# Down groups set apart, moves and taps in three steps, and halved sums in a two-layer decoder trunk

## The chip, the cores and the metric

The kernel runs on one core of a Trainium2 chip. Its engines each work through their own queue in order: PE (TensorE, matrix products; its weight loads are shown as PEld), DVE (VectorE), ACT (ScalarE), POOL (GpSimd) and SP (SyncE, which here only issues DMAs). The metric is the device time of one execution in microseconds (us); lower is better. The time before is 2166.23 us, the median of 3 runs (2166.11 to 2166.46).

## The reference

The input has 256 tokens of 2048 features in float32. Two layers follow each other: one with a pooling mixer, one with dilated attention over a shared K and V. After each mixer comes a gated feed-forward block with a causal convolution of width 3, and after each of the four blocks a layer norm of the scaled stream. The change lies in and around the feed-forward block:

```python
def conv_ffn(h, w_up, conv_w, conv_b, w_down):
    u = h @ w_up
    up = jnp.pad(u, ((0, 0), (CONV_WIDTH - 1, 0), (0, 0)))
    c = conv_b + up[:, 0:S] * conv_w[0]
    for j in range(1, CONV_WIDTH):
        c = c + up[:, j:j + S] * conv_w[j]
    gate, val = jnp.split(c, 2, axis=-1)
    return (jax.nn.silu(gate) * val) @ w_down
...
        h = layer_norm(DEEPNORM_ALPHA * h + mix, ln1_g[i], ln1_b[i])
        ff = conv_ffn(h, ffn_w_up[i], ffn_conv_w[i], ffn_conv_b[i], ffn_w_down[i])
        h = layer_norm(DEEPNORM_ALPHA * h + ff, ln2_g[i], ln2_b[i])
```

`w_up` is 2048 by 11008 (gate and value halves of 5504), `w_down` is 5504 by 2048.

## The kernel before

**Units.** All weights are cut into units, mostly 512 rows by 512 columns (1 MB in float32). The list `units` holds them in the order in which PE takes them, and `run_units` (L125) writes the instructions of every engine unit by unit: `ahead` (L110) issues the load of the unit five further on and the split of the unit three further on; then come the unit's products; then the functions that `later` (L119) has put off to this unit; then the unit's own post function. `later(n, f)` means: n units from here. As every engine keeps this order in its queue, an instruction that waits holds up all that were written behind it on its engine. There are three raw buffers for loads and four buffers for split weights.

**Split.** Every float32 operand is used as a high part (rounded to the matrix format) and a low part (the rest). For a weight unit, `do_split` (L74) lets ACT cast the high part (`wh`, L82) and DVE subtract it from the raw weights (`wl`, L83). Each product is then made as high by high, high by low and low by high. In an up unit (L164 and L165) the activations' two parts lie side by side, so it takes 16 pairs of products of width 512 and 256.

**Seven products.** Down units of certain quads are done with seven block products in place of eight. `split_sums` (L90) makes two units of one weight tile. The "a" unit has ACT cast the left columns and the lower right block (L101) and DVE subtract (L103); then DVE reorders the raw blocks in place by four subtractions (L105 to L108). The "b" unit has ACT cast the whole reordered tile (L95) and DVE subtract it (L96). `mk_seven` (L196) gives three products to the "a" unit and four to the "b" unit (18 and 24 instructions; L223 to L225), the latter in the order: right token block by a left-column block into `t1` (it uses `wh` and `wl` in `N1`), then the sums number 2, 0 and 1 into `s3` and `s2`. The sums of the left operand (`xs`) come from `left_sums` (L617): four additions, and a function one unit later with four casts and four subtractions.

**Feed-forward block.** The 5504 hidden features are cut into quads of four 128-blocks (quad 10 has three). `up(q, mid, end)` (L666) places the gate group of quad q (four up units), then the groups in `mid`, the value group (four up units) and the groups in `end`. After a gate group, `evac` (L564) copies the products out through two scratch buffers (tag `t1`; ACT L576, DVE L577); one unit later `conv` (L580) runs all three taps: four activations for the middle tap (L585), four each for the other two (L590), each pair closed by a DVE addition (L591); one unit later follow sigmoid and product. A value group goes the same way, is multiplied by its gate (L654) and, one unit or more later, is split into the quad tile `gq[q]` (L282, L286), with its left sums. The quads are grouped into chunks (0-2, 3-5, 6-7, 8-10). When a chunk's quads are there, its down products run as four down groups (one for each 512 output columns) between the up groups of the next chunk. A down group of the first two chunks has five units (one ordinary, two pairs of "a" and "b"), one of the third chunk four.

The order around the change, in the first two chunks: gate q, first down group, value q, second down group, gate q+1, third and fourth down group, value q+1. In the third chunk every down group already stands between two up groups. The table `wait` holds back the split of a value quad until the quad tiles of the chunk before are free. After each down group with seven products (of the first three chunks), POOL adds three tiles onto the token stream by accumulating transfers (L267).

**Block moves.** For the down products the stream is turned from features on partitions to tokens on partitions and back: a DVE transpose of 32 by 32 blocks into `hb` and 16 DMAs on SP that put the blocks in place. `to_tokens` (L722) issues its 16 DMAs one unit after the transpose, `to_features` (L743) its 16 in two units, eight each. They are started by `lo` in `chain` (L423) and by `tm_post` (L784). `masks` (L1094) builds the attention masks in the feed-forward block of layer 0.

Of the kernel before, what the change touches and what calls it, by code (L numbers as in the profile page):

```python
# [32 lines left out]
def trunk(ctx: ExitStack, tc: tile.TileContext, x, pool_w_in, pool_w_grp, pool_scale, pool_w_out,  # L33
# [56 lines left out]
    def split_sums(i, kind):  # L90
        h = wh[i] = wp.tile([P, 4, 512], F32R, name=f"wh{i}", tag="wh")
        l = wl[i] = wp.tile([P, 4, 512], F32R, name=f"wl{i}", tag="wl")
        if kind == "b":
            r = raw.pop(i - 1)
            A.copy(h, r)  # L95
            V.tensor_tensor(l, r, h.bitcast(F32), OP.subtract)  # L96
            return
        r = raw[i]
        parts = [(slice(0, 4), N1), (B2, N2)]
        for k, n in parts:  # L100
            A.copy(h[:, k, n], r[:, k, n])  # L101
        for k, n in parts:
            V.tensor_tensor(l[:, k, n], r[:, k, n], h[:, k, n].bitcast(F32), OP.subtract)  # L103
# [3 lines left out]
        V.tensor_tensor(r22, r22, r11, OP.subtract)  # L107
        V.tensor_tensor(r21, r21, r22, OP.subtract)  # L108

    def ahead(i):  # L110
# [77 lines left out]
    def group_tm(w, r0s, c0, ncol, xqs, post, apart=False, seven=(), early=None):  # L188
# [7 lines left out]
        def mk_seven(kind, j):  # L196
            fst, fin, op, cl = j == 0, j == len(r0s) - 1, j == opening, j == closing

            def go(h, l):
# [9 lines left out]
                def sm(i):  # L209
                    return lambda hl, kk: sums[i][:, hl, kk, :]  # L210
# [186 lines left out]
    def chain(ps, lay, which, after):  # L397
# [149 lines left out]
    def ffn(lay):  # L547
# [7 lines left out]
        if lay == 1:  # L555
            sevens[9] = (0, 2)
        wait = {}

# [5 lines left out]
        def evac(ps, nb, mode):  # L564
# [3 lines left out]
            def tmp():  # L568
                return fp.tile([P, T], F32, name="ut", tag="t1", bufs=2)

# [8 lines left out]

        def conv(u, blk0, nb):  # L580
            cv = cvec[lay]
            c = pools["ffn"].tile([P, 4, T], F32, name="c", tag="t4")
            for m in range(nb):
                j = blk0 + m
                A.activation(c[:, m, :], u[:, m, 2:], AF.Identity, scale=cv[:, 2, j:j + 1], bias=cv[:, 3, j:j + 1])  # L585
            a = pools["ffn"].tile([P, 4, T], F32, name="a", tag="t4")
            for i, to in ((1, a), (0, u[:, :, 0:T])):
                for m in range(nb):
                    j = blk0 + m
                    A.activation(to[:, m, :], u[:, m, i:i + T], AF.Copy, scale=cv[:, i, j:j + 1])  # L590
                V.tensor_tensor(c[:, :nb], c[:, :nb], to[:, :nb], OP.add)  # L591
            return c

# [5 lines left out]
        def gate_chain(q, nb, mode, ps):  # L599
                u = evac(ps, nb, mode)  # L600

                def two():
                    c = conv(u, 4 * q, nb)

                    def three():
# [6 lines left out]

                later(1, two)

        def left_sums(q, s):  # L617
            pool, tag = (hp, "h") if q in (2, 5, 7) else (lnp, "sq")
            two = pool.tile([P, 2, 2, 2, P], F32R, name="xs01", tag=tag)
            one = pools["ffn"].tile([P, 2, 2, P], F32R, name="xs2", tag="xs", bufs=2)  # L620
            if len(sevens[q]) < 4:
                own = pools["ffn"].tile([P, 2, 2, P], F32R, name="xs3", tag="xs", bufs=2)
            else:
                own = gq[q][:, 0:2, :, P:T].rearrange("p k h t -> p h k t")
            xs[q] = [two[:, 0], two[:, 1], one, own]
            a11, a12, a21, a22 = (s[:, k:k + 2, t * P:t * P + P] for k, t in ((0, 0), (2, 0), (0, 1), (2, 1)))
# [20 lines left out]
        def val_chain(q, nb, mode, ps):  # L647
            u = evac(ps, nb, mode)

            def two():  # L650
                c = conv(u, NF + 4 * q, nb)

                s = gates.pop(q)
# [7 lines left out]

                later(wait.get(q, 1), three)

            later(0 if q in (2, 5, 7, 10) else 1, two)

# [37 lines left out]
        wait[9] = len(d[3]) - 1  # L703
        up(8, d[:1], d[1:2])
        up(9, d[2:3], d[3:])
        up(10, (), ())
        mark = len(units)
# [14 lines left out]
    def to_tokens(q):  # L722
# [5 lines left out]

        def move():
            ht = hp.tile([P, 4, T], F32, name="ht", tag="h")  # L730
            v = ht.rearrange("p a t -> p (a t)").rearrange("p (t c) -> p t c", t=2)
            to = ht.rearrange("p m t -> p (m t)").rearrange("p (k a j) -> p a k j", k=8, a=4)
            fr = hf.rearrange("p (k b j) -> p b k j", k=8, b=4)
            for a in range(4):
                for b in range(4):
                    nc.sync.dma_start(to[32 * b:32 * b + 32, a], fr[32 * a:32 * a + 32, b])
            HT[q] = v

        later(1, move)

    def to_features(c):  # L743
# [3 lines left out]

        def move(part):
            if part == 0:
                H[c] = hp.tile([P, 4, T], F32, name="h", tag="h")  # L750
            to = H[c].rearrange("p m t -> p (m t)").rearrange("p (k a j) -> p a k j", k=8, a=4)
            fr = hf.rearrange("p (k b j) -> p b k j", k=8, b=4)
            for a in (2 * part, 2 * part + 1):
                for b in range(4):
                    nc.sync.dma_start(to[32 * b:32 * b + 32, a], fr[32 * a:32 * a + 32, b])

        later(1, lambda: move(0))
        later(2, lambda: move(1))


# [23 lines left out]
    def tm_post(lay, n, c):  # L784
# [305 lines left out]
    with tc.tile_pool(name="ffn0", bufs=4) as fp:  # L1090
# [3 lines left out]
        def masks(i):  # L1094
            two = fp.tile([P, 2, P], F32, name="dist", tag="t1", bufs=2)
# [3 lines left out]
            itwo = fp.tile([P, 2, P], I32, name="idist", tag="t1", bufs=2)  # L1099
            idist, im = itwo[:, 0], itwo[:, 1]  # L1100
# [10 lines left out]
        for i in range(3):  # L1111
            later(56 + 3 * i, lambda i=i: masks(i))
        run_units(marks[1])
# [35 lines left out]
```

## Time and profile before

| what | value |
|---|---|
| median of 3 runs | 2166.23 us |
| the profiled execution | 2164.68 us |
| its span, first to last instruction | 2162.9 us |
| DMA traffic | 405.90 MB, mean 188 GB/s |
| casts of whole weight tiles, L82 (ACT, 128x2048) | 286 of 1906 ns |
| subtractions of whole weight tiles, L83 (DVE, 128x2048) | 286 of 2288 ns |

The profile is taken from one execution. Busy time counts an engine's own instructions; matrix products are pipelined, so their durations overlap and PE's busy time says only when it had something in flight. A group's row ends with the engine's idle time just before these instructions and who ended most of it. A window's row gives the busy time of each engine in a stretch, the TensorE clock that was granted there (1.00 is full) and the DMA engines' share. In rows of the timeline, the bracket at the end is the idle time before the instruction and its releaser; "SPq" is SP's DMA queue.

### The profile page before, as it was taken

To read this page: it belongs to the slowest core of one execution; us is meant where nothing else is said; L and a number is where in the kernel's file an instruction comes from. 1 tells how busy PE (TensorE), PEld (TensorE's weight loads), DVE (VectorE), ACT (ScalarE), POOL (GpSimd) and SP (SyncE) were. 2 spreads that over 40 slices of the span, in tenths; PEclk is the share of its full clock that TensorE was granted. 3 is DMA by queue.
4 is the path that set the end of the run, shared out by engine and by line. 5 is a ranking of instruction groups with operands and counts; after the bars stand their busy time and mean duration, and the time that the engine had idled before them with its cause. 6 is when DMAs were issued, how large, how long until landed. Compare 5 with 4: busy or idle time off the path is not lost.

```text
span 2162.9 us, 30852 instructions
## 1 busy us (share of the span) xinstructions
PE 2068.3 (96%) x12388; PEld 1834.3 (85%) x12388; DVE 1678.5 (78%) x1971; ACT 1236.1 (57%) x1612; POOL 75.3 (3%) x112
## 2 busy tenths in 40 slices
PE   9999999898999889989999999999898999899999
PEld 8899987787888788879888888988688888788887
DVE  6768876887888788679856667787788778878878
ACT  6444776565665566456544444576655665665652
POOL 1000000001000000000000000000000000000000
PEclk9999999999999999999999999999999999999999
DMA  8655466556555646675566554557475647546465
GB/s 262 214 181 189 156 196 190 184 190 205 184 166 190 210 149 207 172 213 175 182 203 190 167 193 166 173 177 205 143 229 180 214 154 229 172 149 211 152 205 180
DMA packets 278305, 405.90 MB, mean 188 GB/s; under 512 B 80415, under 2 KB 95669, under 8 KB 277905
## 3 DMA queue, kind: packets, MB, share of 16 engines
q1 hardware_dynamic: 266144, 389.72, 54.2%
q0 software_dynamic: 11584, 13.55, 4.1%
q8 instruction: 97, 1.59, 0.3%
q10 hardware_dynamic: 432, 0.66, 0.1%
q14 instruction: 48, 0.39, 0.1%
HBM read 380.01 MB, written 2.10 MB: 177 GB/s over the span
## 4 chain that ended last, share of the span: by engine, by line
PE 54%; DVE 20%; ACT 15%; DMA 6%; issue 5%; SPq 1%; ACTq 0%; DVEq 0%
PE acc L164 26%; PE acc L165 13%; DVE wl L83 5%; DMA raw<-in_ffn_w_up_dram 4%; ACT wh L95 3%; ACT wh L82 3%; ACT c L585 3%; DVE wl L103 3%; DVE wl L96 2%; PE acc L169 2%; PE acc L168 2%; PE acc L167 2%; ACT a L590 2%; DMA raw<-in_ffn_w_down_dram 2%; ACT u L590 2%
## 5 line engine op out<-in xcount | busy, mean ns | idle before, releaser
L164 PE MATMUL acc<-xc,wh 128*128 128x512 f32 x3264 | 1161.6, 398 | 5.1 <-ACT wh L82 5.0
L165 PE MATMUL acc<-xc,wl 128*128 128x256 f32 x3264 | 922.1, 282 | 21.6 <-DVE wl L83 21.6
L83 DVE TENSOR_TENSOR wl<-raw,wh 128x2048 fp32r<-128x2048 f32 (+2 forms) x326 | 703.1, 2170 | 236.4 <-ACT wh L82 230.2
L82 ACT CAST wh<-raw 128x2048 fp32r<-128x2048 f32 (+2 forms) x326 | 587.0, 1812 | 347.8 <-DMA raw<-in_ffn_w_up_dram 141.5
L164 PEld LDWEIGHTS acc<-xc,wh 128*128 128x128 f32 x3264 | 621.2, 190 | 153.5 <-ACT wh L82 7.3
L165 PEld LDWEIGHTS acc<-xc,wl 128*128 128x128 f32 x3264 | 621.0, 190 | 24.9 <-DVE wl L83 24.8
L95 ACT CAST wh<-raw 128x2048 fp32r<-128x2048 f32 x50 | 95.3, 1906 | 167.7 <-DVE raw L108 157.3
L96 DVE TENSOR_TENSOR wl<-raw,wh 128x2048 fp32r<-128x2048 f32 x50 | 114.6, 2292 | 73.0 <-ACT wh L95 68.9
L576 ACT COPY ut<-acc 128x256 f32<-128x256 f32 x164 | 56.6, 372 | 132.2 <-DVE u L577 120.5
L224 PE MATMUL t<-wl,g 128*128 128x256 f32 x296 | 87.8, 297 | 22.8 <-DVE wl L96 21.2
L223 PE MATMUL t<-wh,g 128*128 128x256 f32 x296 | 85.6, 289 | 22.4 <-ACT wh L95 22.4
L103 DVE TENSOR_TENSOR wl<-raw,wh 128x1024 fp32r<-128x1024 f32 x100 | 91.1, 953 | 11.2 <-ACT wh L101 11.2
L101 ACT CAST wh<-raw 128x1024 fp32r<-128x1024 f32 x100 | 78.5, 834 | 33.8 <-DMA raw<-in_ffn_w_down_dram 16.8
L591 DVE TENSOR_TENSOR c<-c,a 128x1024 f32<-128x1024 f32 (+1 forms) x44 | 52.7, 1198 | 51.0 <-ACT a L590 51.0
L223 PE MATMUL s<-wh,xs 128*128 128x256 f32 x300 | 89.9, 300 | 0.0
L585 ACT ACTIVATE c<-u,cv 128x256 f32<-128x256 f32 x172 | 89.5, 593 | 0.0
L224 PE MATMUL s<-wl,xs 128*128 128x256 f32 x300 | 89.5, 298 | 0.0
L225 PE MATMUL s<-wh,xs 128*128 128x256 f32 x300 | 89.1, 297 | 0.0
L267 POOL DMA_DIRECT2D ht<-w x24 | 20.4, 848 | 1953.2 <-DMA raw<-in_ffn_w_down_dram 679.8
L225 PE MATMUL t<-wh,g 128*128 128x256 f32 x296 | 85.2, 288 | 0.0
L235 PE MATMUL t<-wl,g 128*128 128x512 f32 (+1 forms) x211 | 80.6, 382 | 1.9 <-DVE wl L83 1.9
L234 PE MATMUL t<-wh,g 128*128 128x512 f32 (+1 forms) x211 | 81.2, 385 | 0.6 <-ACT wh L82 0.6
(266 smaller groups left out, 3472.4 us busy)
## 6 DMA issues: line engine op xcount, KB each, us to landing
raw<-in_ffn_w_up_dram SPq DMA_DIRECT2D x160, 1024.0 KB, 4.9
raw<-in_ffn_w_down_dram SPq DMA_DIRECT2D x80, 1024.0 KB, 5.6
raw<-in_pool_w_out_dram SPq DMA_DIRECT2D x16, 1024.0 KB, 5.0
raw<-in_shared_w_k_dram SPq DMA_DIRECT2D x16, 1024.0 KB, 5.0
raw<-in_attn_w_q_dram SPq DMA_DIRECT2D x16, 1024.0 KB, 5.2
raw<-in_shared_w_v_dram SPq DMA_DIRECT2D x16, 1024.0 KB, 5.7
raw<-in_attn_w_o_dram SPq DMA_DIRECT2D x16, 1024.0 KB, 5.0
raw<-in_pool_w_in_dram SPq DMA_DIRECT2D x12, 1024.0 KB, 6.0
```

What stands on the lines that cost most here:

```text
L82: A.copy(wh[i][:, s], r[:, s])
L83: V.tensor_tensor(wl[i][:, s], r[:, s], wh[i][:, s].bitcast(F32), OP.subtract)
L95: A.copy(h, r)
L96: V.tensor_tensor(l, r, h.bitcast(F32), OP.subtract)
L103: V.tensor_tensor(l[:, k, n], r[:, k, n], h[:, k, n].bitcast(F32), OP.subtract)
L164: PE.matmul(ps[m], h[:, k, c], q[:, k, :, :T], start=st, stop=False)
L165: PE.matmul(ps[m][:, :T], l[:, k, c], q[:, k, 0, :T], start=False, stop=sp and not shifted)
L223: PE.matmul(to, xh, h[:, k, n], start=opens and kk == 0, stop=False)
L224: PE.matmul(to, xh, l[:, k, n], start=False, stop=False)
L225: PE.matmul(to, xl, h[:, k, n], start=False, stop=ends and kk == 1)
L585: A.activation(c[:, m, :], u[:, m, 2:], AF.Identity, scale=cv[:, 2, j:j + 1], bias=cv[:, 3, j:j + 1])
L590: A.activation(to[:, m, :], u[:, m, i:i + T], AF.Copy, scale=cv[:, i, j:j + 1])
```

## The change

- `split_sums`: the first reordering moves ahead of the two low-part subtractions of the "a" unit; the reordered blocks come out in other places; the "b" unit is cast and subtracted in two halves of 256 columns, the right half (`N2`) first. `mk_seven` takes the "b" products in the order that goes with it: both `N2` products first, then both `N1` products.
- `conv` is cut into three steps: the middle tap at once, the two other taps one and two units later; what follows (sigmoid, or the product with the gate) hangs on the third.
- Scratch buffers of tag `t1` go from two to four.
- Order of the groups in the first two chunks: gate q, first down group, value q, second, gate q+1, third, value q+1, fourth. The tables `free` and `done` replace `wait`: quads 3, 6 and 9 are split when the fourth down group has ended, and the convolution of the value groups of quads 4 and 7 starts then. The value convolution of quad 7 no longer starts in its own last unit.
- `left_sums` casts and subtracts its first two sums together (three casts and three subtractions in place of four), keeps high and low parts in other layouts, and puts some of them into the layer norm's tiles `S` and `Q`.
- Block moves issue 6, 5 and 5 DMAs in three successive units. Moves to tokens start four units apart instead of three, moves to features four instead of three; the masks come at units 61, 63, 65 in place of 56, 59, 62.

```diff
         if kind == "b":
             r = raw.pop(i - 1)
-            A.copy(h, r)
-            V.tensor_tensor(l, r, h.bitcast(F32), OP.subtract)
+            for n in (N2, N1):
+                A.copy(h[:, :, n], r[:, :, n])
+                V.tensor_tensor(l[:, :, n], r[:, :, n], h[:, :, n].bitcast(F32), OP.subtract)
             return
...
+        V.tensor_tensor(r12, r12, r11, OP.subtract)
         for k, n in parts:
             V.tensor_tensor(l[:, k, n], r[:, k, n], h[:, k, n].bitcast(F32), OP.subtract)
-        r11, r12, r21, r22 = r[:, B1, N1], r[:, B1, N2], r[:, B2, N1], r[:, B2, N2]
-        V.tensor_tensor(r11, r12, r11, OP.subtract)
-        V.tensor_tensor(r12, r22, r12, OP.subtract)
-        V.tensor_tensor(r22, r22, r11, OP.subtract)
+        V.tensor_tensor(r22, r22, r12, OP.subtract)
         V.tensor_tensor(r21, r21, r22, OP.subtract)
+        V.tensor_tensor(r11, r22, r11, OP.subtract)
...
-                    prods = [(a(2, 1), 2, N1, 1, 0, fst, fin), (sm(2), 0, N2, 3, 0, op, False),
-                             (sm(0), 0, N1, 3, 1, False, cl), (sm(1), 2, N2, 2, 1, False, cl)]
+                    prods = [(sm(0), 0, N2, 3, 1, op, False), (sm(1), 2, N2, 2, 1, False, cl),
+                             (a(2, 1), 2, N1, 1, 0, fst, fin), (sm(2), 0, N1, 3, 0, False, cl)]
...
-                later((8, 10, 12, 14)[q], lambda: after(q))
+                later((8, 11, 14, 17)[q], lambda: after(q))
...
-                return fp.tile([P, T], F32, name="ut", tag="t1", bufs=2)
+                return fp.tile([P, T], F32, name="ut", tag="t1", bufs=4)
...
-            a = pools["ffn"].tile([P, 4, T], F32, name="a", tag="t4")
-            for i, to in ((1, a), (0, u[:, :, 0:T])):
+
+            def tap(i, to):
                 for m in range(nb):
                     j = blk0 + m
                     A.activation(to[:, m, :], u[:, m, i:i + T], AF.Copy, scale=cv[:, i, j:j + 1])
                 V.tensor_tensor(c[:, :nb], c[:, :nb], to[:, :nb], OP.add)
-            return c
+
+            def second():
+                tap(1, pools["ffn"].tile([P, 4, T], F32, name="a", tag="t4"))
+
+            def third():
+                tap(0, u[:, :, 0:T])
+                then(c)
+
+            later(1, second)
+            later(2, third)
...
-                for v, src in zip(xs[q], d):
-                    A.copy(v[:, 0], src)
-                for v, src in zip(xs[q], d):
-                    V.tensor_tensor(v[:, 1], src, v[:, 0].bitcast(F32), OP.subtract)
+                both = f[:, 0:2].rearrange("p s (k t) -> p s k t", k=2)
+                vs = [((two[:, :, 0], two[:, :, 1]), both), (xs[q][2], d[2]), (xs[q][3], d[3])]
+                for v, src in vs:
+                    A.copy(v[0], src)
+                for v, src in vs:
+                    V.tensor_tensor(v[1], src, v[0].bitcast(F32), OP.subtract)
...
-                later(wait.get(q, 1), three)
-
-            later(0 if q in (2, 5, 7, 10) else 1, two)
+                at(free.get(q, 0), three)
+
+            after(done.get(q, state["done"] + (0 if q in (2, 5, 10) else 1)), lambda: conv(u, NF + 4 * q, nb, valued))
...
-            wait[q] = sum(len(g) for g in d[1:]) + 3
             up(q, d[:1], d[1:2])
-            up(q + 1, d[2:], ())
+            up(q + 1, d[2:3], d[3:])
+            free[q] = done[q + 1] = len(units) - 1
...
+        for k, (i, n) in enumerate(((0, 6), (6, 5), (11, 5))):
+            later(k + 1, lambda i=i, n=n: part(i, n))
...
-                    later(1 + 3 * q, lambda q=q: to_features(q))
+                    later(1 + 4 * q, lambda q=q: to_features(q))
...
-            later(56 + 3 * i, lambda i=i: masks(i))
+            later(61 + 2 * i, lambda i=i: masks(i))
```

More of the change, by code (lines that the diff above doesn't have):

```diff
@@ L556, in ffn @@
             sevens[9] = (0, 2)
-        wait = {}
+        free, done = {}, {}
         def pads():
@@ L578, in evac, with conv @@
             return u
-        def conv(u, blk0, nb):
+        def conv(u, blk0, nb, then):
             cv = cvec[lay]
@@ L600, in gate_chain, with gated @@
                 u = evac(ps, nb, mode)
-                def two():
-                    c = conv(u, 4 * q, nb)
+                def gated(c):
                     def three():
@@ L611, in two @@
                     later(1, three)
-                later(1, two)
+                later(1, lambda: conv(u, 4 * q, nb, gated))
         def left_sums(q, s):
@@ L648, in val_chain, with valued @@
             u = evac(ps, nb, mode)
-            def two():
-                c = conv(u, NF + 4 * q, nb)
+            def valued(c):
                 s = gates.pop(q)
@@ L702, in ffn @@
         d = down(2, False)
-        wait[9] = len(d[3]) - 1
         up(8, d[:1], d[1:2])
         up(9, d[2:3], d[3:])
+        free[9] = len(units) - 1
         up(10, (), ())
@@ L727, in to_tokens, with to, moves, part @@
         V.transpose(hf.rearrange("p (t m c) -> p m t c", t=2, m=4), H[q].rearrange("p m (t c) -> p m t c", t=2))
[L729 to L739, printed above, removed]
+        def to():
+            HT[q] = hp.tile([P, 4, T], F32, name="ht", tag="h").rearrange("p a t -> p (a t)").rearrange(
+                "p (t c) -> p t c", t=2)
+            return HT[q].rearrange("p t c -> p (t c)")
+        moves(hf, to)
+    def moves(fr, to):
+        fr = fr.rearrange("p (k b j) -> p b k j", k=8, b=4)
+        dst = []
+        def part(i, n):
+            if i == 0:
+                dst.append(to().rearrange("p (k a j) -> p a k j", k=8, a=4))
+            for ab in range(i, i + n):
+                a, b = ab // 4, ab % 4
+                nc.sync.dma_start(dst[0][32 * b:32 * b + 32, a], fr[32 * a:32 * a + 32, b])
+        for k, (i, n) in enumerate(((0, 6), (6, 5), (11, 5))):
+            later(k + 1, lambda i=i, n=n: part(i, n))
     def to_features(c):
@@ L746, in to_features, with to @@
         V.transpose(hf.rearrange("p (m t c) -> p t m c", m=4, t=2), HT[c].rearrange("p t (m c) -> p t m c", m=4))
[L748 to L758, printed above, removed]
+        def to():
+            H[c] = hp.tile([P, 4, T], F32, name="h", tag="h")
+            return H[c].rearrange("p m t -> p (m t)")
+        moves(hf, to)
     def early_post(c, by_dma):
```

25 lines of the change are left out of this document (18 added, 7 removed).

## The prediction

> **What bounds the kernel now.** I read the page's head and its chain of waits, then the granted clock.
>
> ```profile
> span 2162.9 us, 30852 instructions
> PE 2068.3 (96%) x12388; PEld 1834.3 (85%) x12388; DVE 1678.5 (78%) x1971; ACT 1236.1 (57%) x1612; POOL 75.3 (3%) x112
> PE 54%; DVE 20%; ACT 15%; DMA 6%; issue 5%; SPq 1%; ACTq 0%; DVEq 0%
> core 0: 2162.9 us, clock 0.981
> ```
>
> PE sets the end, but it idles 94.6 us (2162.9 - 2068.3), and the chain leaves PE for DVE and ACT for a third of the span. So the next question is where PE waits. The groups by line say it: idle time is the last number.
>
> ```profile
> L165 PE MATMUL acc<-xc,wl 128*128 128x256 f32 x3264 | 922.1, 282 | 21.6 <-DVE wl L83 21.6
> L224 PE MATMUL t<-wl,g 128*128 128x256 f32 x296 | 87.8, 297 | 22.8 <-DVE wl L96 21.2
> L223 PE MATMUL t<-wh,g 128*128 128x256 f32 x296 | 85.6, 289 | 22.4 <-ACT wh L95 22.4
> ```
>
> Nearly half the idle time is the first two products of a "b" unit (the reordered sums), a fifth is an up unit short of its low half. The stretches show where. Columns: window, length, then busy time of PE, PEld, DVE, ACT, POOL, granted clock, DMA share, GB/s.
>
> ```profile
> 240.50:381.50 141.00, 136.86 (x770) 118.90 (x769) 104.91 (x105) 97.72 (x149) 0.00 (x0) 0.99 0.60 185
> 405.90:428.40 22.50, 22.50 (x130) 19.63 (x129) 16.66 (x17) 10.02 (x9) 2.66 (x3) 1.00 0.83 257
> 467.00:507.70 40.70, 34.03 (x219) 31.02 (x218) 34.46 (x39) 22.52 (x28) 2.85 (x4) 0.92 0.49 150
> 639.40:654.80 15.40, 15.40 (x111) 14.32 (x110) 14.47 (x15) 12.67 (x19) 0.00 (x0) 1.00 0.34 112
> 381.50:761.70 380.20, 358.86 (x2146) 318.53 (x2145) 311.93 (x361) 226.29 (x292) 21.55 (x27) 0.97 0.58 188
> 761.70:886.40 124.70, 113.55 (x723) 102.36 (x721) 102.72 (x113) 76.02 (x104) 7.77 (x9) 0.96 0.55 175
> 777.50:803.70 26.20, 24.38 (x128) 20.91 (x129) 23.44 (x24) 12.38 (x12) 2.59 (x3) 0.93 0.70 221
> 803.70:813.90 10.20, 9.96 (x86) 9.76 (x84) 6.92 (x10) 9.54 (x16) 0.00 (x0) 1.00 0.31 104
> 886.40:982.60 96.20, 86.39 (x465) 74.49 (x466) 69.89 (x77) 47.33 (x58) 2.58 (x3) 0.95 0.77 211
> 1407.00:1545.50 138.50, 135.49 (x771) 117.90 (x770) 103.58 (x103) 97.79 (x149) 0.00 (x0) 1.00 0.60 186
> 1545.50:1927.90 382.40, 360.66 (x2145) 320.93 (x2145) 308.56 (x333) 227.85 (x294) 20.70 (x24) 0.97 0.58 187
> 1927.90:2051.10 123.20, 113.47 (x722) 102.42 (x720) 101.54 (x113) 74.95 (x101) 7.77 (x9) 0.96 0.55 178
> 2051.10:2089.00 37.90, 35.57 (x193) 30.80 (x194) 31.22 (x38) 21.25 (x29) 2.58 (x3) 0.95 0.70 222
> ```
>
> Undisturbed, an up group (four units, 128 matmuls) takes 22.5 us, a five-unit down group 15.4, a four-unit one 10.2. From 381.5 to 761.7 run the first two chunks of layer 0: eight down groups and ten up groups, 8 x 15.4 + 10 x 22.5 = 348.2. It takes 380.2: 32.0 lost; in layer 1 382.4: 34.2 lost. The third chunk, four down and three up groups, should take 108.3: 16.4 and 14.9 lost. The two down groups run back to back (467.0 to 507.7) lose 40.7 - 30.8 = 9.9. A loss is stall plus clock: the up group at 777.5 is 3.7 late, 1.8 idle and 1.9 at a low clock.
>
> DVE is busy 311.9 of 380.2 and 102.7 of 124.7, that is 90% and 95% of the undisturbed times. So down groups take more DVE than they give, up groups pay back, and any time DVE spends waiting turns into a PE stall. One such stall closely (start, length, engine and line; at the end the idle time before):
>
> ```profile
> 706.74 0.69 DVE L107 TENSOR_TENSOR raw<-raw 128x512 f32<-128x512 f32 x1
> 707.47 0.69 DVE L108 TENSOR_TENSOR raw<-raw 128x512 f32<-128x512 f32 x1
> 708.27 1.90 ACT L95 CAST wh<-raw 128x2048 fp32r<-128x2048 f32 x1 [7.99 <-DVE raw L108]
> 710.20 2.29 DVE L96 TENSOR_TENSOR wl<-raw,wh 128x2048 fp32r<-128x2048 f32 x1 [2.04 <-ACT wh L95]
> 710.22 0.38 PE L223 MATMUL t<-wh,g 128*128 128x256 f32 x1 [3.10 <-ACT wh L95]
> 712.55 0.58 PE L224 MATMUL t<-wl,g 128*128 128x256 f32 x1 [1.95 <-DVE wl L96]
> 712.92 0.41 PE L225 MATMUL t<-wh,g 128*128 128x256 f32 x1
> ```
>
> DVE finishes the four reorderings, waits 2.04 us for a whole-tile cast, then takes 2.29; PE waits for both and then runs at half speed.
>
> **The change part by part.** What DVE and ACT wait for in total, and the prices:
>
> ```profile
> ACT ut L576 <- DVE u L577: 120.5, 42, 7.5
> DVE wl L96 <- ACT wh L95: 68.9, 44, 2.1
> DVE c L591 <- ACT a L590: 51.0, 30, 3.2
> DVE c L591 <- ACT u L590: 10.7, 30, 0.4
> L96 DVE TENSOR_TENSOR wl<-raw,wh 128x2048 fp32r<-128x2048 f32 x50 | 114.6, 2292 | 73.0 <-ACT wh L95 68.9 <-PE acc L164 4.1
> L103 DVE TENSOR_TENSOR wl<-raw,wh 128x1024 fp32r<-128x1024 f32 x50 | 61.1, 1221 | 11.2 <-ACT wh L101 11.2
> L101 ACT CAST wh<-raw 128x1024 fp32r<-128x1024 f32 x50 | 52.6, 1051 | 33.8 <-DMA raw<-in_ffn_w_down_dram 16.8 <-PE acc L164 14.8 <-PE acc L165 2.0
> ```
>
> *Sums in halves.* In place of one cast of 1.90 and one subtraction of 2.29 come two each; the nearest row for a half is the 128x1024 one, 1.05 and 1.22, the lower bound half of the whole, 1.15 for DVE. So DVE gains nothing or pays 2 x 1.221 - 2.292 = 0.15 per unit; I take 0.15, 7.5 us over 50 units. Against it: the right half needs only the first reorderings, so its cast (1.05) lies under the last two (2 x 0.69) and DVE does not wait. From the last reordering on, the first low half is there after 1.22 and PE begins the two right-half products, against 2.04 + 2.29 + gaps = 4.4 before; the second follows at 2.44, under those products. A stalled unit gains some 3 us at PE, and DVE is free 1.9 earlier. The first reordering also moves ahead of the subtractions, under the casts.
>
> *Taps in three steps.* One conv puts 12 activations on ACT in one unit; DVE waits behind them 51.0 + 10.7 us in 30 convs, 2.1 each, and the next cast stands behind. With four activations per unit, ACT's cast and tap end before DVE's own subtraction: the wait goes, the 2 x 1.2 us of DVE work stays and spreads over later units. Four scratch buffers let ACT copy a group out without DVE; ACT has room (57%), so I price the 120.5 at nothing by itself, as DVE's work covers it; without that cover a cast comes up to 7.5 late. The merged copies of the left sums save under half a microsecond per chunk: nothing.
>
> *Down groups apart.* The fourth group, its three weight loads on SP, its reorderings and its three accumulating transfers on POOL (2.66 us in the row at 405.9) move behind four up units. POOL is idle and the sum is next used a chunk later: no cost. The 9.9 lost in the double stretch need not arise, as each group finds a refilled lead. What is added: the value chain of the group before (taps, casts, sums) is held until the fourth group ends and runs in the next gate group. Behind its first cast on ACT, which waits for PE's last read of the old quad, stand the casts of coming units, on which DVE and then PE depend. PE has three split units in hand then, so I price it at 0; the other end is two units late.
>
> *Moves over three units.* One move is 16 issues on SP:
>
> ```profile
> 337.63 15.55 SPq L736 DMA_DIRECT2D ht<-hb  x16
> 353.28 2.03 SPq L72 DMA_DIRECT2D raw<-in_ffn_w_up_dram  x2
> 359.32 1.91 ACT L82 CAST wh<-raw 128x2048 fp32r<-128x2048 f32 x1 [6.70 <-DMA raw<-in_ffn_w_up_dram]
> ```
>
> The loads queue 15.55 us behind it and ACT waits 6.70. The same issues go out as 6, 5 and 5 with a load between, and moves start four units apart (22.5 us) instead of three (16.9), so SP's 15.55 plus four loads of about 1 us fits, where before it did not. It ends later, but the tokens are wanted after unit 30. The masks move five units, within an up-only stretch: 0.
>
> **The sum.** Against the profiled execution, 2164.7 us (span 2162.9 plus 1.8 around it), 1.5 under the median 2166.2. The chunks lost 32.0 + 34.2 + 16.4 + 14.9 = 97.5. DVE still runs at 90 to 96% there, so I leave one half-tile subtraction (1.22) as stall in 20 of the 24 down groups (some run clean, as at 639.4): 24.4, a gain of 73.1. The lead-in (six up groups, 135.0) lost 6.0 and 3.5, of which I give back half: 4.7. After the third chunk, 456 and 192 matmuls at 22.5 / 128 make 80.2 and 33.8; lost 16.0 and 4.2, to late loads, the last quad and the column-sum chain; half again: 10.1. Together 87.9: 2076.8 in the profile, **2078 us** as median.
>
> One rule speaks for more cost. By the row at 777.5 an idle of 1.8 us came with a low clock. The Trainium skill (TensorE: Matmul & The Clock Gate, Part 1) says the clock halves after at least one idle window of about 3.4 us. By the rule short leftover stalls would cost only themselves, as in my sum; by that row each would cost 1.9 more, which is the first rival.
>
> **Rivals.** *Leftover stalls keep the clock low*: 20 x 1.9 = 38, 2116. For it: the row at 777.5; against: 1.22 is shorter than that stall. *Only the double stretches heal*: DVE stays the bound since its work does not shrink; four times 9.9, 2166.2 - 39.6 = 2127. For it: 95% in the third chunk; against: waits of 68.9 + 61.7 go from DVE's path. *The halves do not do what they say*: if the first cast still waits for all reorderings, 2 x 0.69 comes back in each of about 20 stalled units, 28 us: 2106. Against: the parts of the "a" unit already start separately. *Slower*: the value chain, four units long in place of two, comes too late for the products. Place: the last quad and the last sums before a down stretch, four times a layer, eight in all. For it:
>
> ```profile
> 944.18 0.50 PE L164 MATMUL acc<-g,wh 128*128 128x512 f32 x1 [1.58 <-DVE g L282]
> ```
>
> PE already waited 1.58 us for the last quad of layer 0, and two steps are added to it. Two units (11.2) and 1.9 of clock in eight places is 105: 2078 + 105 = 2183. It decides from 88 / 8 = 11 us per place. Against: in six places four up units lie between.
>
> **Numbers.** Forecast 0.62 (2060 to 2105); low clock 0.14; halves not early 0.06; only double stretches 0.08; too late 0.07; no net change 0.03. Under 0.2% (4 us) a measurement of this kernel tells nothing. Faster 0.90, same 0.03, slower 0.07. Range 2056 (the chunks without any leftover) to 2130 (the third faster rival), leaving out the slower cases.
>
> **What would show it.** The subtraction of the "b" unit waits for ACT under 10 us in total; conv's adds under 15; PE idle under 45 us and clock above 0.99; double stretch replaced by two of 15.4 to 17; the third chunk under 115. Wrong, if PE's idle time moves to the quads or sums (g, xs), to loads, or if DVE's idle time falls and PE's does not.

## The result and the profile after

The changed kernel takes 2058.64 us (median of 4 runs, 2055.07 to 2059.63), the kernel before on the same chip 2166.17. The ratio is 0.9501, with a 95% interval of 0.9484 to 0.9517: 5% faster. The forecast was 2078 us; the gain is 107.5 us where 88 were expected.

Head of the page and granted clock of the changed kernel, profiled at 2059.19 us:

```profile
span 2057.4 us, 30875 instructions
PE 2033.1 (99%) x12388; PEld 1813.7 (88%) x12388; DVE 1668.2 (81%) x2008; ACT 1242.4 (60%) x1649; POOL 75.2 (4%) x112
core 0: 2057.4 us, clock 0.995
```

The products are the same 12388. PE's idle time fell from 94.6 to 24.3 us (2057.4 - 2033.1), 70.3 us; the other 35.2 us of the 105.5 by which the span shrank are PE's busy time, 2068.3 to 2033.1, for the same products. Most of that is the clock, 0.995 in place of 0.981: by this ratio alone the busy time would have shrunk by an estimated 29 us.

The same stretches of the changed kernel (window, length, busy time of PE, PEld, DVE, ACT, POOL, granted clock, DMA share, GB/s):

```profile
241.00:375.90 134.90, 134.90 (x770) 117.84 (x769) 108.16 (x109) 100.23 (x152) 0.00 (x0) 1.00 0.65 199
375.90:724.70 348.80, 348.80 (x2146) 311.80 (x2145) 298.71 (x357) 222.06 (x294) 21.44 (x27) 1.00 0.63 202
724.70:743.80 19.10, 12.23 (x86) 11.41 (x85) 18.29 (x27) 13.79 (x23) 0.00 (x0) 0.91 0.26 85
724.70:841.00 116.30, 109.44 (x723) 100.08 (x722) 109.67 (x131) 81.57 (x117) 7.77 (x9) 0.99 0.62 190
841.00:927.70 86.70, 82.98 (x467) 72.31 (x466) 67.91 (x77) 46.55 (x59) 2.58 (x3) 0.98 0.80 226
1352.20:1487.00 134.80, 134.80 (x770) 117.93 (x769) 108.07 (x109) 100.27 (x152) 0.00 (x0) 1.00 0.64 199
1487.00:1835.90 348.90, 348.90 (x2147) 312.34 (x2146) 292.88 (x327) 222.49 (x294) 20.69 (x24) 1.00 0.63 202
1835.90:1855.50 19.60, 14.22 (x86) 13.22 (x85) 18.79 (x27) 14.31 (x23) 0.00 (x0) 0.74 0.29 97
1835.90:1952.70 116.80, 111.42 (x722) 102.00 (x721) 109.44 (x131) 81.47 (x116) 7.77 (x9) 0.96 0.61 190
1952.70:1986.50 33.80, 33.80 (x195) 29.57 (x194) 27.93 (x35) 20.58 (x29) 2.58 (x3) 1.00 0.76 240
1986.50:2057.40 70.90, 65.81 (x347) 53.97 (x345) 62.60 (x90) 29.82 (x35) 1.72 (x2) 1.00 0.52 175
```

The lead-in (135.0 undisturbed) and the first two chunks (348.2) now run within 0.7 us of that in both layers. The third chunk lost 16.4 and 14.9 and still loses 8.0 and 8.5, all of it in its first down group, which takes 19.1 and 19.6 us for 84 products where 10.2 would do. Added up over both layers, the first two chunks give 64.9 us, the third 14.8, the lead-ins 9.8, the end of layer 0 9.5, the group before the last products 4.1, and the tail of layer 1 behind it 3.0 (73.9 to 70.9).

What PE and DVE wait for in the changed kernel (us in total, times, longest):

```profile
DVE wl L97 <- ACT wh L96: 40.1, 30, 1.9
DVE c L592 <- ACT a L591: 5.9, 14, 1.8
PE s L225 <- DVE wl L106: 4.8, 2, 2.4
PE s L225 <- DVE wl L97: 3.9, 4, 1.6
PE acc L165 <- DVE g L283: 3.7, 1, 3.7
PE t L226 <- DVE u L562: 3.5, 2, 2.1
```

The three large rows of PE's idle time are gone. DVE still waits 40.1 us for the casts of the "b" units (68.9 before), but these are waits of another kind, as a pair of rows of ACT and DVE shows:

```profile
408.42 2.00 ACT L96 CAST wh<-raw 128x1024 fp32r<-128x1024 f32 x2 [4.09 <-PE acc L165]
409.50 2.36 DVE L97 TENSOR_TENSOR wl<-raw,wh 128x1024 fp32r<-128x1024 f32 x2 [1.64 <-ACT wh L96]
```

ACT casts late here because it waits 4.09 us for a product of PE: all four buffers of split weights are full, and PE has to release one. Counted in the trace, 28 of DVE's 30 waits (39.7 of the 40.1 us) stand behind a cast that waited for PE like this one, and none behind a cast that waited for DVE's reorderings. In the kernel before, 26 of 44 waits (50.4 of 68.9 us) stood behind a cast that had waited for DVE. These 28 waits lie in the first two chunks, where PE now loses nothing: a wait with the buffers full is free. A wait in the ring from DVE to ACT and back to DVE, as before the change, uses up what PE has in hand.

The third move to tokens of layer 0 on SP (in the kernel before, its 16 issues took 15.14 us without a load between):

```profile
325.21 3.94 SPq L767 DMA_DIRECT2D ht<-hb  x6
329.78 0.37 SPq L72 DMA_DIRECT2D raw<-in_ffn_w_up_dram  x1
330.20 3.23 SPq L767 DMA_DIRECT2D ht<-hb  x5
335.92 0.37 SPq L72 DMA_DIRECT2D raw<-in_ffn_w_up_dram  x1
336.34 3.29 SPq L767 DMA_DIRECT2D ht<-hb  x5
```

### The profile page after: what moved, and what is told of

Its sections match the earlier page's. It is cut to its first block, busy times and chain, and to the rows that moved or that the text cites. A ratio compares the mean times of both kernels' runs of the same rounds, so it can differ in the third digit from the quotient of the medians.

```text
span 2057.4 us, 30875 instructions
## 1 busy us (share of the span) xinstructions
PE 2033.1 (99%) x12388; PEld 1813.7 (88%) x12388; DVE 1668.2 (81%) x2008; ACT 1242.4 (60%) x1649; POOL 75.2 (4%) x112
## 5 line engine op out<-in xcount | busy, mean ns | idle before, releaser
L96 ACT CAST wh<-raw 128x1024 fp32r<-128x1024 f32 x100 | 101.3, 1050 | 151.5 <-PE acc L165 57.3
L97 DVE TENSOR_TENSOR wl<-raw,wh 128x1024 fp32r<-128x1024 f32 x100 | 118.5, 1221 | 40.1 <-ACT wh L96 40.1
L103 ACT CAST wh<-raw 128x1024 fp32r<-128x1024 f32 x100 | 78.5, 834 | 42.8 <-PE acc L165 36.6
L106 DVE TENSOR_TENSOR wl<-raw,wh 128x1024 fp32r<-128x1024 f32 x100 | 91.1, 954 | 0.0
L237 PE MATMUL t<-wh,g 128*128 128x512 f32 (+1 forms) x211 | 80.9, 383 | 1.0 <-DVE g L283 1.0
L235 PE MATMUL t<-wh,g 128*128 128x512 f32 (+1 forms) x211 | 81.1, 384 | 0.0
L591 ACT ACTIVATE a<-u,cv 128x256 f32<-128x256 f32 x172 | 73.5, 499 | 7.0 <-DVE g L656 7.0
L225 PE MATMUL s<-wl,xs 128*128 128x256 f32 x252 | 72.0, 286 | 3.9 <-DVE wl L97 3.9
L578 DVE TENSOR_TENSOR u<-acc,ut 128x256 f32<-128x256 f32 x164 | 60.0, 416 | 18.4 <-ACT ut L577 18.4
```

The source lines that it names most:

```text
L96: A.copy(h[:, :, n], r[:, :, n])
L97: V.tensor_tensor(l[:, :, n], r[:, :, n], h[:, :, n].bitcast(F32), OP.subtract)
L225: PE.matmul(to, xh, l[:, k, n], start=False, stop=False)
L235: PE.matmul(to, xh, h[:, k, c], start=j == 0 and k == 0, stop=False)
L237: PE.matmul(to, xl, h[:, k, c], start=False, stop=j == len(r0s) - 1 and k == nk - 1)
```

## The experiments

Three accounts were set against each other. *Lead*: DVE's waits, and PE's wait for whole low halves, use up the split units that PE has in hand (its lead). *Adjacency*: the down groups back to back were what mattered. *Scratch*: ACT, held by two copy buffers, was. Times are medians of 4 runs; the kernel before, run beside them, took 2164.2 in the first set (halves, taps, order, scratch buffers), 2168.3 in the second (moves, both single parts, third chunk later) and 2167.2 in the third. As this time moves by 2 us either way, a loss against the 2058.64 us of the changed kernel is uncertain by some 2 to 3 us.

### One part undone

**Halves.** One cast and one subtraction for the "b" unit again:

```diff
-            for n in (N2, N1):
-                A.copy(h[:, :, n], r[:, :, n])
-                V.tensor_tensor(l[:, :, n], r[:, :, n], h[:, :, n].bitcast(F32), OP.subtract)
+            A.copy(h, r)
+            V.tensor_tensor(l, r, h.bitcast(F32), OP.subtract)
```

> The changed kernel with the b unit cast and subtracted whole again (1.91 and 2.29 us), everything else as changed. Theory lead (DVE's waits and PE's wait for the whole low half empty the lead of split units): the subtraction of the b unit again waits some 1.4 us in most of its 50 places, PE stalls at the first b products come back in the five-unit groups and in the third chunk, 2075 to 2110 us. Rival adjacency (the double stretches were what mattered): within 8 us of 2058.6. Rival scratch (the two copy buffers held ACT): within 8 us of 2058.6.

It took 2077.63 us, ratio to before 0.9597 (0.9581 to 0.9613): 19.0 us lost. Windows of this kernel (first two chunks, third chunk of layer 0), then two of its waits:

```profile
375.20:724.00 348.80, 348.80 (x2147) 311.46 (x2146) 295.58 (x341) 219.45 (x277) 21.44 (x27) 1.00 0.63 202
724.00:845.80 121.80, 111.28 (x722) 100.75 (x721) 107.71 (x123) 79.40 (x106) 7.77 (x9) 0.97 0.57 177
```

```profile
DVE wl L96 <- ACT wh L95: 84.6, 42, 2.6
PE s L224 <- DVE wl L96: 13.2, 8, 2.3
```

DVE's wait is back; at 84.6 us it is longer than the 68.9 before the change, though 60.9 us of it stand behind casts that wait for PE. The first two chunks do not notice; the loss is in the third chunk (121.8 against 116.3, 122.0 against 116.8 in layer 1) and in what follows it. The account *lead* had the size right and the place wrong: it expected stalls in the five-unit groups too. The run leaves the first reordering and the order of the products as changed, so it undoes less than the whole part.

**Taps.** `second()` and `third()` called at once in `conv`, and quad 7's value convolution two units later:

```diff
-            later(1, second)
-            later(2, third)
+            second()
+            third()
...
             free[q] = done[q + 1] = len(units) - 1
+            if n == 1:
+                done[q + 1] = len(units) + 1
```

> The changed kernel with all three taps in one unit again (12 activations in a row); the value convolution of quad 7 starts two units later than in the changed kernel, since the tap buffers allow no more, so its quad comes out in the same unit. Lead: conv's additions wait again for ACT, about 60 us in all, part of it in up units with slack, so 2065 to 2085 us. Adjacency and scratch: within 6 us of 2058.6.

2067.63 us, ratio 0.9552 (0.9538 to 0.9566): 9.0 lost, as *lead* expected; conv's additions wait 60.8 us for ACT again. Most of it is again in the third chunk, 121.3 in both layers; the first two chunks lose 2.4 in layer 0. The later start of quad 7 is part of this run and was not tried apart.

**Order.** Third and fourth group back to back, quads 4 and 7 not held:

```diff
-            up(q + 1, d[2:3], d[3:])
-            free[q] = done[q + 1] = len(units) - 1
+            up(q + 1, d[2:], ())
+            free[q] = len(units) - 5
```

> The changed kernel with third and fourth down group back to back again in the first two chunks, and the value convolutions of quads 4 and 7 no longer held back. Adjacency: the four double stretches lose about 10 us each again, 2090 to 2100 us. Lead: with halves and steps a double stretch runs from the lead with little loss, 2058 to 2072 us.

2060.37 us, ratio 0.952 (0.9505 to 0.9534). The interval overlaps that of the changed kernel, so the 1.7 us between the medians are within the uncertainty, and *adjacency* falls as the main cause. Windows of this kernel: a double stretch, the first two chunks, the third:

```profile
452.50:486.30 33.80, 31.84 (x219) 29.06 (x217) 29.98 (x36) 22.24 (x30) 2.58 (x3) 1.00 0.48 141
376.60:733.20 356.60, 350.94 (x2147) 311.79 (x2146) 305.27 (x366) 225.92 (x301) 21.46 (x27) 1.00 0.62 200
733.20:842.00 108.80, 107.56 (x722) 98.48 (x721) 102.34 (x122) 77.20 (x110) 7.77 (x9) 1.00 0.64 198
```

The small net effect hides two of some size. A double stretch now loses 3 us where it lost 9.9 before, and the first two chunks lose 7.8 and 7.7 against the changed kernel. But the third chunk takes 108.8, undisturbed but for 0.5, where the changed kernel takes 116.3. The likely cause is the holding of quad 7's value chain; the run undoes the order and the holding together. So moving the groups apart gains nearly 8 us per layer in the first two chunks and gives it back at the start of the third.

**Scratch buffers.** `bufs=4` back to `bufs=2` for tag `t1`.

> The changed kernel with two scratch buffers instead of four. Scratch: ACT waits about 120 us for DVE again, casts come late and PE stalls, 2075 us or more. Lead and adjacency: ACT's waits come back, but DVE's work covers them, 2056 to 2066 us.

2073.71 us, ratio 0.9582 (0.9567 to 0.9596): 15.1 lost, between the two expectations. The wait in this kernel, then the window of its third chunk:

```profile
ACT ut L577 <- DVE u L578: 91.6, 30, 5.0
```

```profile
726.00:846.70 120.70, 113.08 (x723) 102.36 (x722) 108.00 (x130) 78.50 (x113) 7.76 (x9) 0.96 0.58 181
```

DVE's work does not cover ACT's wait where DVE itself is short of casts: in this third chunk ACT waits 17.2 us for its copy buffers, and DVE 11.1 us for casts (9.0 for whole ones, 2.1 for those of "b" units) where it waits 5.6 in the changed kernel.

**Moves.** 16 issues at once to tokens, 8 and 8 to features, spacings as before:

```diff
-                later((8, 11, 14, 17)[q], lambda: after(q))
+                later((8, 10, 12, 14)[q], lambda: after(q))
...
-                    later(1 + 4 * q, lambda q=q: to_features(q))
+                    later(1 + 3 * q, lambda q=q: to_features(q))
...
-        moves(hf, to)
+        moves(hf, to, ((0, 16),))
```

> The changed kernel with the block moves issued at once again (16 in one unit to tokens, 8 and 8 to features) and started three units apart. If the late loads of the lead-in and the end came from the moves: 5 to 14 us come back, 2063 to 2073 us, at 350 to 375 us and at the end of layer 0. If the other parts leave enough lead to cover them: within 4 us of 2058.6.

2077.42 us, ratio 0.9579 (0.9565 to 0.9593): 18.8 lost, more than either side expected. Windows of the up group after the first down group and of the end of layer 0, then two rows of the timeline:

```profile
393.70:419.90 26.20, 24.36 (x128) 20.91 (x129) 23.91 (x25) 14.89 (x17) 2.65 (x3) 0.93 0.84 260
848.40:944.20 95.80, 84.20 (x468) 72.62 (x467) 68.19 (x77) 46.61 (x59) 2.59 (x3) 0.95 0.75 209
```

```profile
355.15 1.91 ACT L82 CAST wh<-raw 128x2048 fp32r<-128x2048 f32 x1 [7.50 <-DMA raw<-in_ffn_w_up_dram]
911.63 0.79 PE L165 MATMUL acc<-g,wh 128*128 128x512 f32 x1 [9.30 <-DVE g L283]
```

The lead-in itself stays at 134.9. At its end ACT waits 7.50 us for a load, where in the changed kernel the casts of this time wait for PE, so the lead is used up there, and the loss falls due in the next two groups: 1.6 us in the first down group (17.0), 3.7 in the up group shown. The end of layer 0 takes 95.8 in place of 86.7. PE waits 9.30 us there for quad 10. Its value chain shares DVE with the weights' subtractions, which wait 2.36 and 0.38 us for casts, and with a transpose that waits 0.90 us for the move before it; which of these made PE wait was not tried.

### One part alone

The losses of single parts undone add up to 64 us (19.0 + 9.0 + 1.7 + 15.1 + 18.8), the whole change gained 107.5 (the new copies of the left sums were not undone). So two parts were put into the kernel before by themselves. *Halves alone* has the reordering moved ahead, both half loops and the new order of the products:

```diff
+        V.tensor_tensor(r12, r12, r11, OP.subtract)
...
+            for n in (N2, N1):
+                A.copy(h[:, :, n], r[:, :, n])
+                V.tensor_tensor(l[:, :, n], r[:, :, n], h[:, :, n].bitcast(F32), OP.subtract)
```

> The kernel before with the sums in halves alone (reordering first, right half first, products in that order). Theory cover (any one of the parts restores most of the lead in the first two chunks, so each alone is worth far more than undoing it costs): 2085 to 2115 us. Rival sum (parts add up; undoing halves cost 19 us): about 2147 us.

2118.42 us, ratio 0.977 (0.9754 to 0.9786).

*Order alone:*

```diff
-            wait[q] = sum(len(g) for g in d[1:]) + 3
+            wait[q] = sum(len(g) for g in d[1:]) + 7
             up(q, d[:1], d[1:2])
-            up(q + 1, d[2:], ())
+            up(q + 1, d[2:3], d[3:])
...
-            later(0 if q in (2, 5, 7, 10) else 1, two)
+            later({2: 0, 5: 0, 10: 0, 4: 5, 7: 7}.get(q, 1), two)
```

> The kernel before with the down groups apart alone; the value chains of quads 4 and 7 start when the fourth group has ended, that of 7 two units after. Cover: the four double stretches stop losing about 10 us each, less what the held chain costs before the third chunk, 2118 to 2145 us. Sum: undoing the order cost 2 us, so 2160 to 2166 us.

2146.69 us, ratio 0.9898 (0.9883 to 0.9913). First two chunks and third chunk of layer 0, halves alone, then order alone:

```profile
382.20:741.10 358.90, 350.83 (x2147) 311.57 (x2146) 310.29 (x376) 228.66 (x308) 21.52 (x27) 1.00 0.63 199
741.10:863.30 122.20, 112.53 (x722) 102.08 (x721) 103.88 (x121) 77.92 (x112) 7.77 (x9) 0.96 0.57 179
```

```profile
385.20:747.90 362.70, 352.83 (x2147) 314.57 (x2146) 306.64 (x350) 224.45 (x286) 21.50 (x27) 0.98 0.62 196
747.90:876.40 128.50, 114.66 (x722) 103.21 (x721) 106.56 (x122) 78.71 (x110) 7.77 (x9) 0.93 0.55 170
```

Both times lie a little above the range of *cover*, and far from *sum*. Halves are worth 50 us alone and 19 on top of the rest, though these are not quite the same part: the run alone also moves the first reordering ahead and changes the order of the products. In the first two chunks of layer 0 they bring 380.2 down to 358.9, but with whole casts the changed kernel has 348.8 as well. The order is worth 21.6 alone and 1.7, which is not clear of nothing, on top, and it makes the third chunk worse (128.5 against 124.7). The parts cover for each other wherever the lead lasts.

### The stall that is left

In the changed kernel, before the third chunk, both value chains of chunk 6-7 run in the four units of one gate group. The timeline of the changed kernel shows the end of ACT's waiting there, then PE's stalls and the DVE row that ends one of them:

```profile
708.11 2.08 ACT L586 ACTIVATE c<-u,cv 128x256 f32<-128x256 f32 x4 [4.08 <-DVE f L648]
716.91 1.71 ACT L591 ACTIVATE a<-u,cv 128x256 f32<-128x256 f32 x4 [3.51 <-DVE g L656]
...
733.33 0.38 PE L225 MATMUL s<-wl,g 128*128 128x256 f32 x1 [2.38 <-DVE wl L106]
736.79 0.42 DVE L656 TENSOR_TENSOR g<-f,g 128x256 fp32r<-128x256 f32 x1
737.27 0.39 PE L226 MATMUL t<-wh,g 128*128 128x256 f32 x1 [2.13 <-DVE u L562]
739.74 0.58 PE L225 MATMUL s<-wl,xs 128*128 128x256 f32 x1 [1.61 <-DVE wl L97]
```

ACT waits for two tap buffers (tag `t4`), 4.08 and 3.51 us, that quad 6's left sums still hold, and the casts of the coming down units are queued behind it. On DVE, the chain of quad 7 stands between the subtractions of these units. PE idles 6.9 us in the group. 4.7 us of it it waits for low halves of weights (L106, L97). At 737.27 it waits 2.13 us for the low part of the left sum number 3, which DVE makes at 736.79 (L656); the profile puts this wait down to a 0.07 us fill (L562) that ended just after.

**Third chunk later.** Its groups one up group later, moves to features three units apart:

```diff
-        up(8, d[:1], d[1:2])
-        up(9, d[2:3], d[3:])
-        free[9] = len(units) - 1
-        up(10, (), ())
+        up(8, (), d[:1])
+        up(9, d[1:2], d[2:3])
+        up(10, d[3:], ())
+        free[9] = len(units) - 5
```

> The changed kernel with the third chunk's down groups one up group later (first after value 8, second after gate 9, third after value 9, fourth after gate 10), and the moves to features three units apart. If the stall of 9 to 10 us before the third chunk comes from two quads' value chains and left sums pressed into four up units: it goes in both layers, 2036 to 2046 us. If DVE is simply full in the third chunk: the stall moves behind the next group, 2052 to 2062 us.

2058.06 us, ratio 0.949 (0.9475 to 0.9504). The total is in the range of the rival, but its mechanism does not hold: from gate 8 to the fourth group PE is busy throughout, and the loss comes at the end of layer 0. The two windows, then the row of the timeline that carries the loss:

```profile
702.80:850.10 147.30, 146.71 (x946) 132.82 (x945) 136.56 (x165) 104.90 (x153) 10.35 (x12) 1.00 0.65 197
850.10:932.10 82.00, 67.01 (x371) 58.02 (x370) 56.18 (x63) 36.28 (x43) 2.58 (x3) 0.92 0.71 194
```

```profile
899.27 0.80 PE L165 MATMUL acc<-g,wh 128*128 128x512 f32 x1 [13.45 <-DVE g L283]
```

**Quad 10 at once.** The last value group's taps in one unit (`q == 10` calls `second()` and `third()` directly):

> The changed kernel with the taps of the last value group (quad 10) in one unit again, all else as changed. If the 4.0 us stall before quad 10 in layer 0 comes from the two steps added to its chain: the stall shrinks to 2 us or less, 2053 to 2057 us. If late loads and DVE's lag set it: unchanged, 2057 to 2060 us.

2056.48 us, ratio 0.949 (0.9476 to 0.9504), against 2058.64. By the time alone the two cannot be told apart, but the end of layer 0 takes 82.5 in place of 86.7 and PE's wait for quad 10 is gone, as expected if the two added steps made it:

```profile
841.00:923.50 82.50, 81.48 (x468) 71.03 (x467) 67.23 (x76) 46.62 (x59) 2.58 (x3) 1.00 0.85 233
```

**Third chunk later, moves four apart, quad 10 at once:**

> The kernel with the third chunk's groups later in both layers, moves to features four units apart as in the changed kernel (three apart, DVE waited 6.3 and 5.1 us for a move before its transpose and PE 13.5 us for quad 10), quad 10's taps at once. If the spacing made that stall: 2038 to 2046 us. If moves that start four units later collide with the end of layer 0 however they are spaced: 2048 us or more.

2048.51 us, ratio 0.9452 (0.9436 to 0.9467), in the range of the second reading. PE no longer waits for quad 10, but it waits 4.5 us for the sums of the norm after layer 0, with the moves ending later. The run changes the spacing and quad 10's taps at once, so it does not say which of the two took the 13.45 us away.

**The best version** keeps the third chunk as it was in layer 0, with the double stretch in its second chunk so that quad 7 is free early; layer 1 has the third chunk later; quad 10 at once:

```diff
+            if lay == 1 or n == 0:
+                up(q + 1, d[2:3], d[3:])
+                free[q] = done[q + 1] = len(units) - 1
+            else:
+                up(q + 1, d[2:], ())
+                free[q], done[q + 1] = len(units) - 5, len(units) - 1
...
+        cut = 1 - lay
+        up(8, d[:cut], d[cut:cut + 1])
+        up(9, d[cut + 1:cut + 2], d[cut + 2:cut + 3])
+        up(10, d[cut + 3:], ())
+        free[9] = len(units) - (9 if lay == 0 else 5)
```

> The changed kernel with three places mended: quad 10's taps at once; in layer 1 the third chunk's down groups one up group later; in layer 0 the third and fourth group of the second chunk back to back, so that quad 7's chain need not be held. If the held chain of quad 7 costs the 9 to 10 us per layer: the stall at the third chunk's first group falls to 1 us in both layers, at 4 us for the double stretch, 2038 to 2047 us. If DVE is simply full there: 2050 us or more.

2046.87 us (2045.63 to 2049.05), ratio 0.9446 (0.9432 to 0.946), below the changed kernel's 0.9501 with intervals apart, but not to be told apart from the 0.9452 of the version just above. Third chunk of layer 0, then of layer 1 (here with the gate groups 8 and 10 in it):

```profile
730.10:839.00 108.90, 107.64 (x723) 98.55 (x722) 102.42 (x122) 77.37 (x111) 7.77 (x9) 1.00 0.67 199
1807.30:1954.70 147.40, 146.67 (x947) 132.89 (x946) 136.61 (x165) 105.01 (x153) 10.36 (x12) 1.00 0.65 197
```

The third chunk is undisturbed in both layers with DVE just as busy (102.4 of 108.9 us), so DVE was not simply full there: the two value chains were squeezed. The time is at the upper edge of what was expected; the tail of layer 1 grew from 70.9 to 75.8. The last down products now follow the third chunk's closely, which may be why; it was not tried.

## Why the prediction was right, and what it mis-sized

- *What bounds the kernel.* Right: the 105.5 us came out of PE's idle time (70.3) and its busy time at a low clock (35.2), in the stretches named, with DVE's total work nearly unchanged (1678.5 to 1668.2 us). The forecast was 17.6 us short of it in the profile (87.9). Every term was too small: the chunks by 6.6, the ends of the layers by 3.5, the lead-ins by 5.1, and the tail by all of its 3.0; the rest of the kernel took 0.6 longer.
- *The chunks*, 73.1 expected, 79.7 measured (64.9 + 14.8). The leftover was taken as one short stall in 20 of 24 groups, 24.4 us. 17.8 were left, but 22 groups have next to none and two have 9 us each. That the sum came near is luck; the mechanism behind that term did not happen. DVE's 90 to 96% of PE's time was read as a sign of stalls to come. It is none: with the order undone and in the best version DVE is busy 94% of the third chunk, which loses only 0.5 or 0.6 us.
- *Sums in halves.* The direction held: PE's waits at the first products of the "b" units fell from 43.6 us (22.4 + 21.2) to 3.9, by the whole change. The sign was wrong: DVE's wait was to be under 10 us and is 40.1, because it now waits with all split buffers full. What has gone is the wait for its own reorderings. The part is worth 19 us in this company and 50 alone.
- *Taps in three steps.* Conv's additions wait 5.9 us where under 15 was forecast; undone, with quad 7 shifted, the part costs 9.0.
- *Scratch buffers*, priced at nothing, cost 15.1 us when taken away. The step that failed is "DVE's work covers it": in the third chunk DVE then waits 11.1 us for casts in place of 5.6, because ACT, held at the copies, casts late.
- *Down groups apart.* The first two chunks gain nearly 8 us per layer by it in the presence of the other parts, not 19.8 (two times 9.9). The held value chain was priced at 0, "PE has three split units in hand then". That step failed too: the third chunk takes 7.5 and 7.8 us more than with the order undone, as the coming units are split behind the chain on ACT and DVE. The slower rival's mechanism, a chain too late for its own products, shows in two of its eight places for sums (2.13 and 1.41 us) and in one for quad 10 (3.7 us against 1.58 before). It was far from deciding.
- *Moves.* The lead-ins gave 9.8, twice the 4.7 in the sum, and the ends 13.6 against 10.1. Half of the loss, given back by judgement, was too little in both. Undoing the moves alone costs 18.8 us, but in layer 0 none of it in the lead-in: it falls due behind it.
- *The tail* of layer 1 gave 3.0 us that the sum did not have.
- *The range.* Its lower end, 2056, was called the chunks without any leftover; by the terms given this is 2053.6 (2078 less 24.4). The upper end, 2130, is the rival worth 2127, rounded up. The measured 2058.64 lies inside either way, close to the lower end.
- *Rivals.* "Leftover stalls keep the clock low" did not come true as a whole, yet its rule was half right. With the order undone, a double stretch lost 3 us in stalls under 1 us each at a clock of 1.00. But where longer stalls stand close together the clock fell: 0.91 in the stretch at 724.7, 0.74 in its twin of layer 1 at 1835.9. One gap settles nothing: in the kernel before, a single one of 1.94 us (it ends at 612.60) was followed by 3 us of products of 0.41 us in place of 0.28, and in the changed kernel the gap of 2.38 at 733.33 was followed by none, its twin of 2.37 in layer 1 (at 1844.32) by products of 0.42 us almost to the end of the group. So stalls of this length can cost more than themselves, against the sum; what decides stays open. "Only the double stretches heal" falls with the order undone (2060.37). That the halves might not start early was not seen: in the changed kernel no wait of DVE stands behind a cast that waited for all reorderings, and with halves alone DVE waits 7.4 us in all for their casts.

What stays open is how the 107.5 us divide between the parts: the runs show that they cover for each other, and no single figure belongs to each.

## What to carry to other kernels

Where a busy helper engine feeds the bound engine through a few buffers, ask of each stretch how much lead it starts with, not how long the helper waits in total. A wait behind a full set of buffers is free, a wait that empties them is not; look at what the engine that is waited for was itself waiting for. One fix hides the next. Undo parts of a finished change to see what still matters, and add them singly to see what they could do; the two differ (19 and 50 us for the halves here). Work that is put off to spare one stretch lands in another: check that the one after has room, and that its temporary buffers are not still held.

## What was not expected of the hardware

The issues of a block move do not all take the same time. SP's queue in the kernel before, first and third move to tokens of layer 0:

```profile
288.61 10.55 SPq L736 DMA_DIRECT2D ht<-hb  x16
...
319.90 15.14 SPq L736 DMA_DIRECT2D ht<-hb  x16
```

The same 16 issues took 0.66 us each in the first move and 0.95 in the third; the four moves took 10.55, 11.70, 15.14 and 15.55 us. In the changed kernel they took 11.27, 10.39, 10.46 (3.94 + 3.23 + 3.29, shown above) and 13.00 us, and with the moves undone 11.64, 14.70, 14.47 and 16.59. So the first move is no shorter in three parts and the fourth is still slow, but the four together took 45.1 in place of 52.9 us. What slows the later issues, and whether the loads between or the wider spacing helped, was not tried.
